# New transfer and GpSimd prices in a one-core decoder trunk's scheduler, with edits to a layer norm and a block-diagonal store

## The chip, the cores and the metric

One core of a Trainium2 chip runs the whole program. The time is the device time of one launch in microseconds (us). The kernel before was run three times.

## The reference, cut to what matters

Two post-norm layers over 1024 positions of width 1024, all in float32. Layer 0 mixes with a gated DeltaNet (8 heads of 128, chunks of 64), layer 1 with an S5 state-space scan; beside each runs a 4-head attention into 256 memory tokens. Each layer ends in a squared-ReLU MLP of 4096. The layer norms are the part that the change touches most plainly:

```python
def layer_norm(x, g, b):
    mu = jnp.mean(x, axis=-1, keepdims=True)
    var = jnp.mean(jnp.square(x - mu), axis=-1, keepdims=True)
    return (x - mu) * lax.rsqrt(var + 1e-5) * g + b
...
for i in range(2):
    mix, xq = gdn_mixer(x, ...) if i == 0 else s5_mixer(x, ...)
    cross = memory_attention(xq, mem, w_kv[i])
    h = jnp.concatenate([mix, cross], -1) @ w_o[i]
    x = layer_norm(ALPHA * x + h, ln1_g[i], ln1_b[i])
    f = jnp.square(jax.nn.relu(x @ mlp_w1[i])) @ mlp_w2[i]
    x = layer_norm(ALPHA * x + f, ln2_g[i], ln2_b[i])
```

Inside the DeltaNet a unit lower triangular system of 64 x 64 is solved per chunk and head. The kernel inverts the 32 x 32 diagonal blocks of it first.

## The kernel before, in words

**Matmuls.** A float32 product is three matmuls on rounded parts: every operand x is split into xh (ScalarE casts it to fp32r) and xl = x - xh (VectorE), and `mm3` (L397, L398, L399) adds xh*yh, xl*yh, xh*yl into one PSUM bank. The large products also use a seven-product scheme, whose sums and differences of blocks are formed on VectorE (`s`, `a1`, `u`, `p`, `hid`, L599, L690, L696, L768) and go through DRAM scratch (`hd`, `wsd`, `wod`, `osd`). A block is 128 x 512 float32, 256 KB.

**Stages by time in the profile.** Projections and memory keys (to 200 us), the DeltaNet's heads in recurrence with the next head's projections woven in (to 700), output projection with layer norm 1 and the first MLP blocks (700 to 810), the first MLP with the S5 tables and coefficients beside it (to 1380), layer norm 2 (to 1450), the S5 scan, attention and gate (to 1700), and the same output projection, layer norm and MLP for layer 1. The last 8 row tiles of 128 x 1024 (`mlp_last`) each get two half accumulations `tm`, which VectorE adds into `y` (L931), then `layer_norm`, then a store of the tile to the output.

**What sets the order.** The code only records instructions. `settle` (L62, called once at the end of `run`, L2277) then simulates the five queues with prices from `price` (L293) and writes out one order per engine, which is fixed by dependencies without semaphores. It takes, at each step, the instruction that can start soonest, and among those the one that is due first; TensorE's own recorded order is kept within `reach=40` us, others may start up to `ahead=70` us before they are due. A transfer's price is a length of 1.6 us plus its size over 300 GB/s (2 us more from GpSimd, 0.7 more for short runs), and `late` is added to when its data are there: a 256 KB load from SyncE is counted as 1.6 + 0.85 + `late`. `late` isn't part of when something is due. An engine executes its queue strictly in order, so an instruction whose operand isn't there holds up all that stand behind it.

**Layer norm (L493).** Two forms. The one of layer norm 1, with `junk`, sums on ScalarE (L502 for the mean, L505 for the squares, each over two halves), finishes the statistics on VectorE (L503, L506), and uses a gain that was multiplied by 32 beforehand (L2302), as it works with the sum over 1024 in place of the mean. The one of layer norm 2, without `junk`, takes VectorE's statistics (L509 twice, L510), adds 1e-5 on GpSimd (L511) and raises to -1/2 on GpSimd (L512). Then VectorE applies (y - mean) * gain (L515) and y * rstd + bias (L516).

**The diagonal blocks.** `gdn_keys_out` runs 16 times (8 heads, 2 halves). It leaves NT, the strict lower part, 4 tiles of 128 x 128. ScalarE copies the four 32 x 32 diagonal blocks into `pkd` (L1157, four copies of 32 x 128), and GpSimd issues one store of `pkd` to `ntd` (L1158) and one of the whole NT to `ntf` (L1159). `gdn_inverse` reads `ntd` for two heads at a time. On the same GpSimd queue stand the powers for the keys' and outputs' norms (L1140, L1452).

Of the kernel before, what the change touches and what calls it, by code (L numbers as in the profile page):

```python
# [20 lines left out]
HALF = 512  # L21
# [12 lines left out]
class Trunk:  # L34
# [258 lines left out]
    def price(self, i, big):  # L293

        E = mybir.EngineType
        if i.opcode == "DMACopy":
            def run(ap):
                k = 1
                for s, c in reversed(ap):
                    if s != k:  # L300
                        break
                    k *= c
                return 4 * k

# [12 lines left out]
        slow = 1.65 if any(s > 1 and c > 1 for s, c in q) else 1.0  # L317
        scalars = any(math.prod(c for s, c in x.bass_ap.ap[1:]) == 1 for x in i.ins if getattr(x, "bass_ap", None) is not None) and big > 1
        if i.engine == E.Activation:
            bank = self.home.get(i.ins[0].bass_ap.tensor.name, "s")[0] == "ps"  # L320
            if i.opcode == "TensorCopy":
                t = (0.05 if bank else 0.096) + 0.84e-3 * big * slow
            else:
                t = (0.08 if bank else 0.125) + 0.8e-3 * big + (0.08 if len(i.outs) > 1 else 0.0) + (0.07 if scalars else 0.0)
            return t, t + 0.1, 0
        if i.engine == E.Pool:
            t = 0.02 + 0.87e-3 * big if i.opcode == "Memset" else 0.5 if big < 2 else 1.0 if big < 8 else 0.17 + 2.1e-3 * big
            return t, t + 0.05, 0
        wide = sum(c > 1 for x in i.ins if getattr(x, "bass_ap", None) is not None for c in [math.prod(c for s, c in x.bass_ap.ap[1:])])
        if getattr(i, "is_tensor_tensor_scan", False):  # L330
            return 2.46e-3 * big, 2.46e-3 * big + 0.08, 0
        t = 0.07 + (0.53e-3 if i.opcode == "TensorScalarPtr" and wide < 2 else 1.04e-3) * big * slow + (0.06 if scalars and i.opcode == "TensorScalarPtr" else 0.0)
        return t, t + 0.08, 0
# [156 lines left out]
            out.append(t)  # L490
        return out

    def layer_norm(self, y, gb, junk=None):  # L493

        nc = self.nc
        st = self.tile("st", [P, 2, 6], F32, "bn")
        halves = y if isinstance(y, list) else [y[:, c * HALF:(c + 1) * HALF] for c in range(2)]
        mv = self.tile("st", [P, 4], F32, "mv")
        if junk is not None:
            s = st.rearrange("p a b -> p (a b)")  # L500
            for c in range(2):
                nc.scalar.activation(junk, halves[c], AF.Copy, accum_out=s[:, c:c + 1])  # L502
            nc.vector.tensor_scalar(mv[:, 0:1], s[:, 0:1], s[:, 1:2], -1.0 / 1024, op0=ALU.add, op1=ALU.mult)  # L503
            for c in range(2):
                nc.scalar.activation(junk, halves[c], AF.Square, bias=mv[:, 0:1], accum_out=s[:, 4 + c:5 + c])  # L505
            nc.vector.scalar_tensor_tensor(mv[:, 2:3], s[:, 4:5], s[:, 5:6], self.eps_ln, op0=ALU.add, op1=ALU.add)  # L506
        else:
            for c in range(2):
                nc.vector.bn_stats(st[:, c, :], halves[c])  # L509
            nc.vector.bn_aggr(mv[:, 0:2], st)  # L510
            nc.gpsimd.tensor_scalar(mv[:, 2:3], mv[:, 1:2], 1e-5, None, op0=ALU.add)  # L511
        nc.gpsimd.tensor_tensor(mv[:, 3:4], mv[:, 2:3], self.mhalf[:, 0:1], op=ALU.pow)  # L512
        parts = [(y, slice(0, 1024))] if not isinstance(y, list) else [(y[c], slice(c * HALF, (c + 1) * HALF)) for c in range(2)]
        for o, c in parts:
            nc.vector.scalar_tensor_tensor(o, o, mv[:, 0:1], gb[0][:, c], op0=ALU.subtract if junk is None else ALU.add, op1=ALU.mult)  # L515
            nc.vector.scalar_tensor_tensor(o, o, mv[:, 3:4], gb[1][:, c], op0=ALU.mult, op1=ALU.add)  # L516
# [603 lines left out]
    def gdn_keys_out(self, h, hf):  # L1120


        nc = self.nc
        V = nc.vector
        kT = self.kTs[h % 4]
        t4 = slice(4 * hf, 4 * hf + 4)
# [21 lines left out]
        n = self.tile("h1", [P, 4, P], F32, "NT")  # L1148
        for t in range(4):
            tt = 4 * hf + t  # L1150
            c = slice(tt * P, (tt + 1) * P)
            nc.tensor.matmul(pq[:, t, :], kT[:, c], kT[:, c], start=True, stop=True)
        V.scalar_tensor_tensor(n, pq, -1.0, d, op0=ALU.mult, op1=ALU.mult)
        pkd = self.tile("S", [P, 4, 32], F32, "pkd")
        for b in range(4):
            q = slice(32 * b, 32 * b + 32)
            nc.scalar.copy(pkd[q], n[q, :, q])  # L1157
        nc.gpsimd.dma_start(self.ntd[h, t4].rearrange("t b j i -> (b j) t i"), pkd)  # L1158
        nc.gpsimd.dma_start(self.ntf[h, hf], n)  # L1159

    def gdn_inverse(self, h0):
# [1041 lines left out]
    def run(self):  # L2203
        nc = self.nc
# [69 lines left out]
        for _ in steps:  # L2274
            pass
        self.mlp_block(1, B, ahead, self.x3, None, a["out"].rearrange("(n s) d -> s n d", s=8), None)
        self.settle(self.begin, self.nc.cur_bb.bb.instructions[-1], reach=40.0, ahead=70.0, margin=0.2, late=0.7)  # L2277

    def rows(self, src):

# [54 lines left out]
    def mlp_block(self, i, B, ahead, xd, side, out, more):  # L2335
        new = []

        def done(y, tau):
            if tau == 0:
                self.gb2 = self.load_gb(self.a["ln2_g"][i:i + 1], self.a["ln2_b"][i:i + 1])  # L2340
                if more:
                    new.extend(self.new_xT())
            self.layer_norm(y[tau], self.gb2)
            self.nc.sync.dma_start(out[tau], y[tau])
            if more and tau == 7:
                self.last_x(y, new, more(new))
            elif more and tau < 6:
                self.transpose_x(y[tau], tau, new)

        self.mlp_first(i, B, ahead, side)  # L2350
        self.mlp_second(i, xd, done, side)
        return new
# [87 lines left out]
```

## Time and profile before

| | |
|---|---|
| median of 3 runs | 2513.91 us (2511.46 to 2515.65) |
| the profiled execution, its time | 2513.31 us |
| its span | 2511.6 us (1.7 us lie around it) |
| TensorE busy | 2472.5 us, 98% of the span |
| VectorE busy | 1973.9 us, 79% |
| ScalarE busy | 1294.0 us, 52% |
| GpSimd busy | 420.7 us, 17% |
| moved by DMA | 481.18 MB |
| granted TensorE clock, mean | 0.999 |

How to read it: TensorE is busy nearly all the time, so what can be lost or won is the time in which it waits, 39 us of 2512, and what it takes from its last matmul to the end. The view of waits lists, for each engine, whom an instruction waited for with its sum, count and longest; a timeline row has its start and length, engine, line, operation, output<-inputs, and in brackets the idle time of the engine just before it with what ended it.

### The profile page before, as it was taken

Reading aid. Unit: us, or ns where it says so; the run is one execution under the profiler, and the core shown is the slowest. Engines: PE = TensorE matmul, PEld = TensorE weight load, DVE = VectorE, ACT = ScalarE, POOL = GpSimd, SP = SyncE. Lnnn points to the kernel's source line nnn. Section 1 sums busy time; section 2 is a strip of 40 time slices with the busy share of each in tenths; the row PEclk is TensorE's granted clock in tenths of the full one; section 3 lists DMA queues with packets and bytes.
Section 4 is the critical chain, followed back from the end, with each engine's and each line's share of the span. In section 5 each row is a group of like instructions: output and inputs, shape, how many; then the busy total and the mean of one; then the engine's idle time right before and its main releaser. Section 6 shows DMA issues by size and latency. Waiting matters only on the chain.

```text
span 2511.6 us, 36963 instructions
## 1 busy us (share of the span) xinstructions
PE 2472.5 (98%) x12181; PEld 2060.4 (82%) x12181; DVE 1973.9 (79%) x3663; ACT 1294.0 (52%) x2776; POOL 420.7 (17%) x641
## 2 busy tenths in 40 slices
PE   8999999999999999999999999999999999999998
PEld 6888888888887887888888888888887888888886
DVE  7786878888779798879988957776687666578788
ACT  6665565554456566554444244564365555544441
POOL 0132232314002023312210223112011000000001
PEclk9999999999999999999999999999999999999999
DMA  6453575767754567477454479669736444574532
GB/s 215 119 166 119 141 238 152 234 199 238 262 163 151 198 206 242 166 283 242 141 161 143 156 242 305 200 220 330 258 130 202 159 143 164 213 261 130 168 105 97
DMA packets 319089, 481.18 MB, mean 192 GB/s; under 512 B 109440, under 2 KB 139344, under 8 KB 318896
## 3 DMA queue, kind: packets, MB, share of 16 engines
q1 hardware_dynamic: 292912, 423.76, 51.5%
q0 software_dynamic: 23680, 50.85, 7.0%
q10 hardware_dynamic: 2304, 4.20, 0.5%
q8 instruction: 96, 1.57, 0.3%
q14 instruction: 97, 0.79, 0.1%
HBM read 321.91 MB, written 156.73 MB: 191 GB/s over the span
## 4 chain that ended last, share of the span: by engine, by line
PE 87%; DVE 5%; ACT 3%; DMA 2%; issue 2%; POOL 1%; SPq 0%; POOLq 0%; DVEq 0%; ACTq 0%
PE q L398 7%; PE q L399 7%; PE q L397 7%; PE pA L399 4%; PE pA L397 4%; PE pA L398 4%; PE tm L397 4%; PE tm L398 4%; PE tm L399 4%; PE wi L397 3%; PE wi L399 3%; PE wi L398 3%; PE pC L399 2%; PE pC L397 2%; PE pC L398 2%
## 5 line engine op out<-in xcount | busy, mean ns | idle before, releaser
L397 PE MATMUL q<-wkh,hkh 128*128 128x512 f32 x784 | 306.2, 391 | 0.8 <-ACT G L1881 0.8
L398 PE MATMUL q<-wkl,hkh 128*128 128x512 f32 x784 | 306.0, 390 | 0.5 <-DVE wkl L894 0.5
L399 PE MATMUL q<-wkh,hkl 128*128 128x512 f32 x784 | 305.3, 390 | 0.0
L893 ACT CAST wkh<-wr 128x512 fp32r<-128x512 f32 x168 | 104.8, 624 | 238.0 <-PE q L398 185.8
L397 PEld LDWEIGHTS q<-wkh,hkh 128*128 128x128 f32 x784 | 147.2, 188 | 32.5 <-ACT G L1881 1.7
L398 PEld LDWEIGHTS q<-wkl,hkh 128*128 128x128 f32 x784 | 147.2, 188 | 31.1 <-DVE wkl L894 1.1
L399 PEld LDWEIGHTS q<-wkh,hkl 128*128 128x128 f32 x784 | 147.2, 188 | 30.2
L894 DVE TENSOR_TENSOR wkl<-wr,wkh 128x512 fp32r<-128x512 f32 x168 | 115.4, 687 | 65.6 <-issue 56.5
L397 PE MATMUL wi<-xTh,wih 128*128 128x512 f32 x384 | 158.0, 411 | 1.6 <-ACT qT L1091 1.6
L398 PE MATMUL wi<-xTl,wih 128*128 128x512 f32 x384 | 153.1, 399 | 0.0
L399 PE MATMUL wi<-xTh,wil 128*128 128x512 f32 x384 | 152.9, 398 | 0.0
L894 DVE TENSOR_TENSOR hkl<-hr,hkh 128x512 fp32r<-128x512 f32 x196 | 133.8, 683 | 0.1
L893 ACT CAST hkh<-hr 128x512 fp32r<-128x512 f32 x196 | 120.8, 616 | 2.6 <-DMA hr<-hd 2.6
L511 POOL TENSOR_SCALAR mv<-mv 128x1 f32<-128x1 f32 x16 | 9.0, 565 | 631.6 <-DVE mv L510 631.6
L397 PE MATMUL tm<-so 128*128 128x512 f32 x280 | 110.3, 398 | 0.4 <-ACT so L1616 0.4
L1616 ACT CAST so<-or 128x1024 fp32r<-128x1024 f32 x70 | 71.9, 1051 | 61.4 <-DMA or<-wod 40.0
L1617 DVE TENSOR_TENSOR so<-or,so 128x1024 fp32r<-128x1024 f32 x70 | 84.3, 1220 | 19.4 <-ACT so L1616 17.4
L399 PE MATMUL tm<-so 128*128 128x512 f32 x224 | 87.8, 393 | 0.0
L398 PE MATMUL tm<-so 128*128 128x512 f32 x224 | 87.7, 392 | 0.0
L397 PEld LDWEIGHTS wi<-xTh,wih 128*128 128x128 f32 x384 | 72.9, 190 | 14.4 <-ACT qT L1091 2.0
L399 PEld LDWEIGHTS wi<-xTh,wil 128*128 128x128 f32 x384 | 72.6, 189 | 14.0
L398 PEld LDWEIGHTS wi<-xTl,wih 128*128 128x128 f32 x384 | 72.8, 190 | 11.8 <-issue 0.2
(582 smaller groups left out, 7389.8 us busy)
## 6 DMA issues: line engine op xcount, KB each, us to landing
hr<-hd SPq DMA_DIRECT2D x212, 256.0 KB, 2.8
wr<-in_w_dram SPq DMA_DIRECT2D x56, 512.0 KB, 4.8
hd<-u SPq DMA_DIRECT2D x92, 256.0 KB, 2.0
w1r<-in_w_dram SPq DMA_DIRECT2D x32, 512.0 KB, 3.6
hd<-hid SPq DMA_DIRECT2D x60, 256.0 KB, 2.4
hd<-p SPq DMA_DIRECT2D x60, 256.0 KB, 2.1
w1r<-in_w_dram SPq DMA_DIRECT2D x56, 256.0 KB, 3.6
wir<-in_w_in_dram SPq DMA_DIRECT2D x24, 512.0 KB, 4.0
```

The lines of the kernel that those rows point to most:

```text
L397: mm(ps, a[0], b[0], start=start, stop=False, skip_group_check=onto)
L398: mm(ps, a[0], b[1], start=False, stop=False, skip_group_check=onto)
L399: mm(ps, a[1], b[0], start=False, stop=stop, skip_group_check=onto)
L511: nc.gpsimd.tensor_scalar(mv[:, 2:3], mv[:, 1:2], 1e-5, None, op0=ALU.add)
L893: nc.scalar.copy(hi, s)
L894: nc.vector.tensor_tensor(lo, s, f32(hi), op=ALU.subtract)
L1616: nc.scalar.copy(hi, r)
L1617: V.tensor_tensor(lo, r, f32(hi), op=ALU.subtract)
```

## The change

Three kinds of edits are made at once.

1. Prices. `late` goes from 0.7 to 1.5 us, so each transfer is taken to land 0.8 us later. A GpSimd tensor-tensor operation on one column is priced 0.9 us in place of 0.5.
2. Layer norm 2. The `1e-5` step moves from GpSimd to VectorE and works on 1024 times the variance (the gain is multiplied by 32 on ScalarE, once per layer). In layer 1, tiles 5 and 6 use the form with ScalarE's sums, with a free PSUM bank as scratch. The very last tile applies the bias in two halves, each with a store of its own.
3. Diagonal blocks. The copies into `pkd` are gone; four stores per call take the blocks out of NT directly.

```diff
         if i.engine == E.Pool:
-            t = ... else 0.5 if big < 2 else 1.0 if big < 8 else 0.17 + 2.1e-3 * big
+            t = ... else (0.9 if i.opcode == "TensorTensor" else 0.5) if big < 2 else 1.0 if big < 8 else 0.17 + 2.1e-3 * big
...
-    def layer_norm(self, y, gb, junk=None):
+    def layer_norm(self, y, gb, junk=None, last=None):
...
             nc.vector.bn_aggr(mv[:, 0:2], st)
-            nc.gpsimd.tensor_scalar(mv[:, 2:3], mv[:, 1:2], 1e-5, None, op0=ALU.add)
+            nc.vector.tensor_scalar(mv[:, 2:3], mv[:, 1:2], 1024.0, 1024 * 1e-5, op0=ALU.mult, op1=ALU.add)
         nc.gpsimd.tensor_tensor(mv[:, 3:4], mv[:, 2:3], self.mhalf[:, 0:1], op=ALU.pow)
+        if last is not None:
+            nc.vector.scalar_tensor_tensor(y, y, mv[:, 0:1], gb[0], op0=ALU.subtract, op1=ALU.mult)
+            for c in range(2):
+                c = slice(c * HALF, (c + 1) * HALF)
+                nc.vector.scalar_tensor_tensor(y[:, c], y[:, c], mv[:, 3:4], gb[1][:, c], op0=ALU.mult, op1=ALU.add)
+                nc.sync.dma_start(last[:, c], y[:, c])
+            return
...
-        pkd = self.tile("S", [P, 4, 32], F32, "pkd")
         for b in range(4):
             q = slice(32 * b, 32 * b + 32)
-            nc.scalar.copy(pkd[q], n[q, :, q])
-        nc.gpsimd.dma_start(self.ntd[h, t4].rearrange("t b j i -> (b j) t i"), pkd)
+            nc.gpsimd.dma_start(self.ntd[h, t4, b].rearrange("t j i -> j t i"), n[q, :, q])
...
-        self.settle(..., reach=40.0, ahead=70.0, margin=0.2, late=0.7)
+        self.settle(..., reach=40.0, ahead=70.0, margin=0.2, late=1.5)
...
                 self.gb2 = self.load_gb(self.a["ln2_g"][i:i + 1], self.a["ln2_b"][i:i + 1])
+                self.nc.scalar.activation(self.gb2[0], self.gb2[0], AF.Copy, scale=32.0)
...
-            self.layer_norm(y[tau], self.gb2)
-            self.nc.sync.dma_start(out[tau], y[tau])
+            self.layer_norm(y[tau], self.gb2, self.psum("mm", "jk") if tau in ((), (5, 6))[i] else None, last=out[tau] if tau == 7 and not more else None)
+            if tau < 7 or more:
+                self.nc.sync.dma_start(out[tau], y[tau])
```

The count of TensorE's instructions stays the same. Its order is the same for most of the program: of every hundred matmuls, ten stand more than seven places from where they stood, mostly in the DeltaNet's recurrence and around the two layer norms 1. The other engines' orders are reshuffled locally. Line numbers after the edits are 5 to 7 higher (L599 becomes L606, L573 L580, L931 L938, L516 L523, L1140 L1147, L1159 L1164).

**VectorE in the first MLP, near 932 us.** Before, `hid` is added to `p` between the two sums `s` of one coefficient, and the low part `a1l` comes behind:

```order
L765 TENSOR_TENSOR p_1829_10445<-pB_10556,p_1829_10445 128x512
L696 TENSOR_TENSOR s_1837_10521<-w1r_10517,w1r_10518 128x512
L599 TENSOR_TENSOR hid_10489<-hid_10489,p_1794_10224 128x512
L690 TENSOR_TENSOR s_1838_10523<-s_1837_10521,w1r_10515 128x512
L573 TENSOR_TENSOR a1l_10526<-w1r_10515,a1h_10525 128x512
L573 TENSOR_TENSOR s1l_10530<-s_1837_10521,s1h_10529 128x512
L768 TENSOR_TENSOR u_1831_10475<-pA_10432,u_1831_10475 128x512
```

The same block of the first MLP (same tiles under new numbers) in the changed kernel's VectorE queue:

```order
L703 TENSOR_TENSOR s_1821_10489<-w1r_10485,w1r_10486 128x512
L772 TENSOR_TENSOR p_1813_10413<-pB_10524,p_1813_10413 128x512
L697 TENSOR_TENSOR s_1822_10491<-s_1821_10489,w1r_10483 128x512
L580 TENSOR_TENSOR a1l_10494<-w1r_10483,a1h_10493 128x512
L580 TENSOR_TENSOR s1l_10498<-s_1821_10489,s1h_10497 128x512
L775 TENSOR_TENSOR u_1815_10443<-pA_10400,u_1815_10443 128x512
L606 TENSOR_TENSOR hid_10457<-hid_10457,p_1778_10192 128x512
```

The step on `hid` moved from ahead of `a1l` to behind it. This holds in some blocks and is reversed in others.

**VectorE at the end of the program.** `tm` is a half accumulation from TensorE, `mv_24311` belongs to tile 6 and `mv_24349` to tile 7, the last. Before:

```order
L515 SCALAR_TENSOR_TENSOR y_21743<-y_21743,mv_24311,gb_24078 128x1024
L931 TENSOR_TENSOR y_21743<-tm_24320,y_21743 128x512
L516 SCALAR_TENSOR_TENSOR y_21743<-y_21743,mv_24311,gb_24080 128x1024
L509 BN_STATS bn_24348<-y_21743 128x6
L931 TENSOR_TENSOR y_21743<-tm_24334,y_21743 128x512
L509 BN_STATS bn_24348<-y_21743 128x6
L510 BN_AGGR mv_24349<-bn_24348 128x2
L515 SCALAR_TENSOR_TENSOR y_21743<-y_21743,mv_24349,gb_24078 128x1024
L516 SCALAR_TENSOR_TENSOR y_21743<-y_21743,mv_24349,gb_24080 128x1024
```

In the changed kernel the same queue ends like this (`mv_24285` is tile 6's, `mv_24325` tile 7's):

```order
L503 TENSOR_SCALAR mv_24285<-bn_24284 128x1
L938 TENSOR_TENSOR y_21712<-tm_24296,y_21712 128x512
L509 BN_STATS bn_24324<-y_21712 128x6
L506 SCALAR_TENSOR_TENSOR mv_24285<-bn_24284,eps_ln 128x1
L522 SCALAR_TENSOR_TENSOR y_21712<-y_21712,mv_24285,gb_24047 128x1024
L938 TENSOR_TENSOR y_21712<-tm_24310,y_21712 128x512
L523 SCALAR_TENSOR_TENSOR y_21712<-y_21712,mv_24285,gb_24049 128x1024
L509 BN_STATS bn_24324<-y_21712 128x6
L510 BN_AGGR mv_24325<-bn_24324 128x2
L514 SCALAR_TENSOR_TENSOR y_21712<-y_21712,mv_24325,gb_24047 128x1024
L511 TENSOR_SCALAR mv_24325<-mv_24325 128x1
L517 SCALAR_TENSOR_TENSOR y_21712<-y_21712,mv_24325,gb_24049 128x512 x2
```

Tile 6's bias step (L523) now stands behind the last addition of `tm` and still ahead of the last tile's statistics; the variance step L511 stands behind the 1024-wide L514.

**GpSimd in the DeltaNet's recurrence, fourth head.** Before:

```order
L1159 DMA ntf<-NT_2451 128x512
L1158 DMA ntd<-pkd_2457 128x4x32
L1140 TENSOR_TENSOR scr_79<-scr_79,half 128x4
L1452 TENSOR_TENSOR scr_79<-scr_79,mhalf 128x4
L1159 DMA ntf<-NT_2553 128x512
L1158 DMA ntd<-pkd_2559 128x4x32
```

After:

```order
L1163 DMA ntd<-NT_2439 32x4x32 x4
L1164 DMA ntf<-NT_2439 128x512
L1147 TENSOR_TENSOR scr_79<-scr_79,half 128x4
L1457 TENSOR_TENSOR scr_79<-scr_79,mhalf 128x4
L1163 DMA ntd<-NT_2539 32x4x32 x4
L1164 DMA ntf<-NT_2539 128x512
```

Four issues stand where one stood, ahead of the store of NT instead of behind it, and the powers follow them.

More of the change, by code (lines that the diff above doesn't have):

```diff
@@ L326, in price @@
         if i.engine == E.Pool:
-            t = 0.02 + 0.87e-3 * big if i.opcode == "Memset" else 0.5 if big < 2 else 1.0 if big < 8 else 0.17 + 2.1e-3 * big
+            t = 0.02 + 0.87e-3 * big if i.opcode == "Memset" else (0.9 if i.opcode == "TensorTensor" else 0.5) if big < 2 else 1.0 if big < 8 else 0.17 + 2.1e-3 * big
             return t, t + 0.05, 0
@@ L2276, in run @@
         self.mlp_block(1, B, ahead, self.x3, None, a["out"].rearrange("(n s) d -> s n d", s=8), None)
-        self.settle(self.begin, self.nc.cur_bb.bb.instructions[-1], reach=40.0, ahead=70.0, margin=0.2, late=0.7)
+        self.settle(self.begin, self.nc.cur_bb.bb.instructions[-1], reach=40.0, ahead=70.0, margin=0.2, late=1.5)
     def rows(self, src):
```

## The prediction

> **What bounds the kernel now.** I read the page first, then the busy time by stage, then TensorE's waits, then the timeline at the longest waits and at the end. The page says who is full:
>
> ```profile
> span 2511.6 us, 36963 instructions
> PE 2472.5 (98%) x12181; PEld 2060.4 (82%) x12181; DVE 1973.9 (79%) x3663; ACT 1294.0 (52%) x2776; POOL 420.7 (17%) x641
> ```
>
> TensorE is idle for 2511.6 - 2472.5 = 39.1 us. The change leaves its 12181 matmuls as they are, so their 2472.5 us stay, and only the 39 us can move much. Where they lie, from the view by stretches (start:end, length, then busy time of PE, PEld, DVE, ACT, POOL):
>
> ```profile
> 0.00:10.00 10.00, 2.47 (x6) 1.23 (x7) 3.33 (x8) 4.38 (x6) 1.76 (x14) 1.00 0.74 261
> ...
> 200.00:600.00 400.00, 391.69 (x2208) 330.81 (x2207) 324.66 (x668) 223.80 (x713) 121.00 (x186) 1.00 0.63 183
> ...
> 700.00:810.00 110.00, 107.09 (x517) 86.13 (x517) 91.83 (x144) 66.96 (x139) 20.90 (x18) 1.00 0.48 158
> ...
> 900.00:1000.00 100.00, 96.85 (x425) 79.16 (x424) 90.38 (x243) 66.53 (x118) 37.84 (x68) 1.00 0.71 228
> ...
> 2460.00:2512.00 52.00, 41.91 (x185) 34.36 (x184) 46.07 (x65) 0.00 (x0) 10.69 (x16) 0.93 0.20 81
> ```
>
> 7.5 us are the start (the change doesn't reach it), 10.1 us the end. The middle holds 39.1 - 7.5 - 10.1 = 21.5 us: 8.3 in the DeltaNet's recurrence, 2.9 at layer norm 1, 3.2 in the first MLP's tables, some 7 spread over the rest. The granted clock is full in all of them. TensorE's waits, the longest in total (sum, times, longest):
>
> ```profile
> PE pA L399 <- DVE a1l L573: 3.1, 2, 1.7
> PE wi L397 <- ACT qT L1091: 1.6, 1, 1.6
> PE pA L399 <- DVE w1l L364: 1.5, 2, 1.0
> ...
> PE wz L397 <- ACT vT L1091: 1.3, 2, 0.8
> ...
> PE pS L1436 <- ACT e L1432: 1.1, 3, 0.7
> ```
>
> No single wait exceeds 1.7 us, and each ends with VectorE or ScalarE coming late to an operand. These two are busy for 79% and 52%, so this is lateness in an in-order queue and no lack of engine. That is what another order can mend, or make.
>
> **The change part by part.**
>
> *Transfers counted as landing later.* The scheduler counts 1.6 + 0.85 + 0.7 = 3.15 us for a 256 KB load from SyncE before, 3.95 after; for 512 KB 4.0 and 4.8. What they took (size, median us from issue to landing):
>
> ```profile
> hr<-hd SPq DMA_DIRECT2D x212, 256.0 KB, 2.8
> wr<-in_w_dram SPq DMA_DIRECT2D x56, 512.0 KB, 4.8
> or<-wod SPq DMA_DIRECT2D x40, 256.0 KB, 3.7
> x<-y SPq DMA_DIRECT2D x32, 256.0 KB, 2.1
> ```
>
> The old price fits the quick ones, the new price the slow ones. The longest wait of the profile, at 932 us, shows what a slow one does:
>
> ```profile
> 932.17 0.69 DVE L599 TENSOR_TENSOR hid<-hid,p 128x512 f32<-128x512 f32 x1 [1.59 <-DMA hd<-hid]
> 932.78 0.68 DVE L690 TENSOR_TENSOR s<-s,w1r 128x512 f32<-128x512 f32 x1
> 933.38 0.68 DVE L573 TENSOR_TENSOR a1l<-w1r,a1h 128x512 fp32r<-128x512 f32 x1
> ...
> 934.12 0.50 PE L399 MATMUL pA<-xB,a1l 128*128 128x512 f32 x1 [1.68 <-DVE a1l L573]
> ```
>
> VectorE stands 1.59 us before `hid`, because an earlier store of that buffer hasn't been read out; behind it stand the second `s` and `a1l`, and TensorE waits 1.68 us for `a1l`. In the new order `hid` stands behind `a1l`: 1.59 us of the 1.68 go. What is late next there is `hid` itself, which only stores a sum, so nothing near it waits. Term: -1.6 us. Against it stands that in other blocks, three in this MLP and four in the second at most, `hid` now stands two to four places ahead of `a1l` where it was behind. A store that is late there would cost the same 1.6 us; before, three blocks stood so and one waited. For the rest of the middle I take a smaller value: the waits on `w1l` (1.5) and the second one on `a1l` (1.4) lie behind loads or tables and gain at most the 0.8 us by which their estimates grow, so from -1.6 to 0 for the two, and +1.6 if the order swaps them for others. I take -0.8.
>
> *The diagonal blocks.* Rows of the tiles `pkd` and `ntd`, and of 32-partition loads on GpSimd's queue (duration in ns: least, median, most):
>
> ```profile
> L1157 ACT COPY pkd<-NT x64: 280/295/300, 53.6 to 507.5; 32x128 f32<-32x128 f32 x64
> L1158 POOL DMA_DIRECT2D ntd<-pkd x16: 750/762/824, 60.4 to 508.1; - x16
> ...
> L1274 POOL DMA_DIRECT2D iv<-t x64: 548/549/615, 156.4 to 591.7; - x64
> ```
>
> ScalarE loses 64 x 0.295 = 18.9 us of work, all between 54 and 508 us. Each group of four held its queue for 1.18 us just after NT, ahead of evacuations like `qT`, `vT` and `e`, for which TensorE waits 1.6 + 1.3 + 1.1 = 4.0 us in this stage. GpSimd gains: four issues at 0.549 are 2.20 in place of 0.762, +1.43 us, 16 times, +22.9 us in a stage where it is busy for 121 of 400 us. Along the path from NT to `ntd` the two cancel (1.18 + 0.76 before, 2.20 after). Four ScalarE copies less ahead of the evacuations is worth between 0 and the 4.0 us; an evacuation is behind such a group only some of the time, and the reshuffle of this stage (where TensorE's own order moves most) can also cost. I take -2.5. Cover for GpSimd's longer issues is its idle 70%; where the powers L1140 and L1452 stand right behind them, that cover is gone and each costs up to 1.43 us (a rival, below).
>
> The Trainium skill's page "SBUF — State Buffer", section "SBUF: two separate sides", speaks against putting more issues on GpSimd: while VectorE runs an operation that takes both ports, GpSimd cannot write its descriptors, and the transfer starves. The rows of L1274 don't show that: with VectorE busy for 325 of 400 us, the longest of 64 issues took 0.615 against a median of 0.549, so by the trace the sum stays as it is.
>
> *Layer norm 2 and the end.* The last tile before, and TensorE's last matmul of the last two halves:
>
> ```profile
> 2498.80 0.39 PE L399 MATMUL tm<-w2h,hk 128*128 128x512 f32 x1
> ...
> 2501.52 0.39 PE L399 MATMUL tm<-w2h,hk 128*128 128x512 f32 x1
> ```
>
> ```profile
> 2502.99 0.68 DVE L931 TENSOR_TENSOR y<-tm,y 128x512 f32<-128x512 f32 x1
> ...
> 2504.43 0.21 DVE L510 BATCH_NORM_AGGREGATE mv<-bn 128x2 f32<-128x12 f32 x1
> 2504.67 1.28 DVE L515 SCALAR_TENSOR_TENSOR y<-y,mv,gb 128x1024 f32<-128x1024 f32 x1
> 2504.73 1.31 POOL L511 TENSOR_SCALAR mv<-mv 128x1 f32<-128x1 f32 x1 [3.58 <-DVE mv L510]
> 2506.12 0.57 POOL L512 TENSOR_TENSOR mv<-mv,mhalf 128x1 f32<-128x1 f32 x1
> 2506.72 1.28 DVE L516 SCALAR_TENSOR_TENSOR y<-y,mv,gb 128x1024 f32<-128x1024 f32 x1 [0.77 <-POOL mv L512]
> 2508.03 0.33 SPq L2344 DMA_DIRECT2D out_dram<-y  x1
> ```
>
> The last addition starts 1.1 us after TensorE ends (2501.9), since VectorE is still at tile 6. From L510 to L516 it takes 2.29 us. In the new order L511 stands on VectorE behind the 1024-wide L514: 0.24 to L514, 1.2 for it, 0.2 for L511, about 0.3 to GpSimd, 0.57 for the power: 2.5 us, so moving L511 gains nothing here, because it was put behind the operation that blocked it before. Tiles 5 and 6 now go through ScalarE, whose steps have these lengths (layer norm 1's rows; squares of two halves, then VectorE):
>
> ```profile
> 779.58 0.72 ACT L505 ACTIVATE tw<-y,mv 128x512 bf16<-128x512 f32 x1
> ...
> 781.05 0.19 ACT L505 ACTIVATION_READ_ACCUMULATOR tw<-y,mv 128x1 f32 x1
> ...
> 781.27 0.22 DVE L506 SCALAR_TENSOR_TENSOR mv<-bn,eps_ln 128x1 f32<-128x1 f32 x1 [0.77 <-ACT tw L505]
> ```
>
> 1.7 us for the squares, by the same kind of pass some 0.8 for the sum of the half that came last, and 0.3 at each handover. TensorE makes a half in 2501.52 - 2498.80 = 2.72 us, so tile 6's second half is there at 2496.5. VectorE reaches its addition behind tile 5's two 1.2 us steps, about 2498.0 by these lengths; the sum is ready at 2499.5, the squares at 2501.5, L522 ends at 2502.8. Then in order the last addition (0.6), tile 6's L523 (1.2), half the statistics (0.6), L510 at 2505.3 instead of 2504.4, and with 2.5 us the first L517 at 2507.8. Its second half ends at 2509.0 (2508.0 before), but its store has 256 KB, 2.1 us against 2.7 for 512 KB by the kinds of rows above (the second, by its group):
>
> ```profile
> x<-y SPq DMA_DIRECT2D x8, 512.0 KB, 2.7
> ```
>
> Term: +1.0 - 0.6 = +0.4 us. Bounds: -0.8 if VectorE is at tile 6 as soon as TensorE, +1.5 if each ScalarE handover costs 0.3 more. In layer 0 the same step moves and the extra gain scaling is one 128 x 1024 pass per layer, asked for tens of us after its load: nothing, with 0.5 us either way.
>
> *Sum.* -1.6 - 0.8 - 2.5 + 0.4 = -4.5 us by the parts that I can name. To this I add -1.2 for the other 7 us of scattered waits, a sixth of them, on the ground that a later landing only ever moves a consumer back behind work that is ready; between -4 and +4, since an order can also put two late things in a row. That is -5.7. The profiled execution took 2513.31, 0.6 us below the median: 2513.31 - 5.7 = 2507.6, and 2508.2 against the median. I say 2508.0. About 0.2% (5.0 us: 2508.9 to 2518.9 is no change) is what a measurement of this kernel can tell from nothing.
>
> **The rivals.**
>
> *The waits only change places* (2513 us, 2509 to 2519). For it: TensorE's order is nearly the old one, all gains are of 1 or 2 us, the end gives a little back, and half of the 21.5 us (layer norms' serial chains, the recurrence) isn't about transfers. Against it: the one wait whose rows I could follow in the new order goes.
>
> *GpSimd's queue becomes the wait* (slower). Place: 200 to 600 us, the powers behind the four issues. Price 1.43 us each, up to 22.9 us for 16. It decides by the number of calls in which a power is asked for within 1.43 us behind the issues: four such calls (4 x 1.43 = 5.7) eat the whole gain, eight (11.4 against 5.7 + 5.0 = 10.7) make it slower than can be mistaken. If ScalarE's 2.5 us don't come either, nine give 12.9 - 5.7 + 2.5 = +9.7, 2523 us, and twelve 2527. For it: both powers follow directly in the new order. Against it: GpSimd is 70% idle there, and the scheduler prices these issues at 0.6 us, above the rows' 0.549, so it has planned for them.
>
> *`hid` ahead of `a1l`* (slower). Seven blocks times 1.6 us is 11.2, less the 1.6 won: 2523 us, with half of them 2518. Against it: one of three waited before, and only where the tables' transfers were thick.
>
> **How the numbers follow.** Waits shrink as summed, by 5 us or more: 0.40, with a range of its own of 2499 to 2508.9. Places change: 0.33. GpSimd's queue: 0.15. `hid` and like collisions: 0.12. So faster 0.40, the same 0.33, slower 0.27. The low end of the range is the sum with the best value of each part: -1.6 - 1.6 - 4.0 - 0.8 - 4 = -12, 2501.5, which I round to 2501; the upper end is 2523, where both slower cases have their middle. About 1 in 10 is left out on each side.
>
> **What would show it.** Right: no wait of over 1 us for `a1l` in the first MLP; less than 6 us idle between 200 and 600; L511 on VectorE behind L514 and the last store 2.1 us long; the end between 9 and 11 us after TensorE's last matmul. Wrong: TensorE idle for 10 us or more between 200 and 600, with the powers' starts on GpSimd pushed behind the stores of the blocks; new waits for `a1l` behind `hid`; or more idle time at the layer norms 1 than the 2.9 us.

## The result: 13 us slower

| | before | after |
|---|---|---|
| median | 2514.36 us (6 runs, 2511.46 to 2515.65) | 2527.49 us (6 runs, 2524.97 to 2528.06) |
| profiled execution, its span | 2513.31, 2511.6 us | 2527.54, 2525.8 us |
| TensorE's last matmul ends at | 2501.9 us | 2515.9 us |
| granted TensorE clock, mean | 0.999 | 0.994 |

The ratio is 1.0053, 95% interval 1.0042 to 1.0064: slower by 10.6 to 16.1 us. Forecast were 2508.0 us and, at most, 2523.

The page of the changed kernel, its first lines:

```profile
span 2525.8 us, 36952 instructions
PE 2479.4 (98%) x12181; PEld 2069.0 (82%) x12181; DVE 1975.3 (78%) x3676; ACT 1289.0 (51%) x2732; POOL 435.8 (17%) x673
```

The same 12181 matmuls are busy for 6.9 us more (2479.4 against 2472.5), and TensorE is idle for 46.4 us where it was idle for 39.1. A busy time that grows without more work is the first thing to see: some of the matmuls ran slower. The stretches, as in the prediction:

```profile
200.00:600.00 400.00, 390.23 (x2181) 332.18 (x2179) 320.71 (x666) 211.04 (x668) 129.01 (x208) 0.99 0.64 186
700.00:810.00 110.00, 106.56 (x507) 87.16 (x506) 90.10 (x139) 66.03 (x141) 21.75 (x19) 0.97 0.47 158
900.00:1000.00 100.00, 100.00 (x443) 82.81 (x442) 94.08 (x249) 69.97 (x124) 38.07 (x71) 1.00 0.74 237
2460.00:2526.00 66.00, 55.24 (x243) 45.10 (x241) 57.59 (x91) 14.57 (x31) 7.26 (x8) 0.96 0.24 93
```

The first MLP's tables (900 to 1000) are now full, as forecast; the granted clock (third number from the end) is below 1.00 in two stages where it was full, and layer norm 1 (700 to 810) is idle for 3.4 us instead of 2.9. TensorE's waits, from the same view as before:

```profile
PE ba L1011 <- ACT xTh L993: 7.6, 2, 7.3
PE ks L1429 <- DVE S L1446: 4.4, 2, 3.6
PE tm L397 <- ACT so L1621: 3.7, 1, 3.7
PE xt L530 <- DVE xB L535: 3.0, 3, 1.5
PE tm L397 <- DVE y L894: 1.9, 2, 1.2
PE tm L399 <- DVE ow L1654: 1.7, 1, 1.7
```

The waits for `a1l` and `w1l`, together 4.6 us before, are gone from the head of the list. In their place stand two of 3.6 and 3.7 us, where nothing in the middle of the program had waited longer than 1.7.

**Where the 14 us arise.** The starts of the same matmul in both traces, subtracted (us; the first column is its time before; the next is how much later it starts in the changed kernel):

| matmul | before | after | e1 edits only | e2 late back | e4 prices only | e9 chain early |
|---|---|---|---|---|---|---|
| last `ks` of the recurrence | 691.7 | +4.8 | +1.3 | +2.9 | +6.0 | +3.7 |
| last `xt` of layer 0 (norm 1 done) | 804.3 | +7.3 | +1.0 | +3.1 | +8.4 | +6.0 |
| first `wu` (layer 1 begins) | 1431.7 | +2.6 | -1.0 | -0.3 | +5.4 | +0.9 |
| first `so` product of layer 1 | 1750.2 | +3.7 | -1.9 | -0.7 | +6.5 | +1.3 |
| last `xt` of layer 1 | 1909.0 | +13.4 | -2.3 | +1.2 | +16.5 | +1.3 |
| end of the last matmul | 2501.9 | +14.0 | -2.5 | +1.1 | +17.1 | +2.2 |

So the changed kernel loses 4.8 us in the recurrence and 2.5 in the first output projection with layer norm 1, wins 4.7 back in the first MLP, loses 1.1 in the S5 part, and then loses 9.7 us in the second output projection alone. (e1 to e9 are experiments, below. Executions differ by up to 2.4 us in such a row even with the same work in the same order: +4.8, +7.2 and +6.1 at the last `ks` for the changed kernel, e5 and e11, whose TensorE runs the same list up to there. One difference shows: a power on GpSimd near 441 us took 1.1 us in the changed kernel's profile and 3.2 us in the other two.)

**The wait near 1795 us.** The timeline of the changed kernel, rows of SyncE's queue, VectorE, ScalarE and TensorE in order of time:

```profile
1777.86 0.43 SPq L623 DMA_DIRECT2D ws<-cat  x1
...
1784.17 0.68 DVE L630 TENSOR_TENSOR ws<-ws,ws 128x512 f32<-128x512 f32 x1
...
1784.88 0.32 SPq L635 DMA_DIRECT2D osd<-ws  x1
...
1789.65 0.32 SPq L1615 DMA_DIRECT2D or<-osd  x1
1790.01 0.43 SPq L1616 DMA_DIRECT2D or<-wod  x1
...
1794.76 1.04 ACT L1621 CAST so<-or 128x1024 fp32r<-128x1024 f32 x1 [12.02 <-DMA or<-wod]
...
1795.86 0.51 PE L397 MATMUL tm<-so 128*128 128x512 f32 x1 [3.70 <-ACT so L1621]
```

It is a chain: four blocks are loaded into `ws`, VectorE forms the seven-product scheme's sums in place (L630 to L633), SyncE stores them to the scratch `osd`, and half of the product's operand `or` is loaded back from there (the other half comes from `wod`, one issue behind). The product that waits reads the first of this last group's four sums. Before, the same chain (other line numbers) had this time:

```profile
1764.58 0.43 SPq L616 DMA_DIRECT2D ws<-cat  x1
...
1771.40 0.68 DVE L623 TENSOR_TENSOR ws<-ws,ws 128x512 f32<-128x512 f32 x1
...
1772.12 2.06 SPq L628 DMA_DIRECT2D osd<-ws  x2
...
1776.21 0.47 SPq L1611 DMA_DIRECT2D or<-wod  x1
...
1782.90 0.50 PE L397 MATMUL tm<-so 128*128 128x512 f32 x1 [0.35 <-ACT so L1616]
```

The last load into `ws` is issued 13.3 us later than before, the first sum and its store come 12.8 us later, the load of `or` 13.8 us, and TensorE starts the product 13.0 us later; only 3.7 of these were there when the stage began. From the first sum to the product it takes 11.7 us, 11.5 before: inside this group next to nothing is lost. The delay had grown over the groups ahead, which go through the same few `ws` buffers: the first sums of the five groups stand at 1711.5, 1725.3, 1738.9, 1756.0 and 1771.4 before, and 6.9, 11.8, 17.2, 13.4 and 12.8 us later in the changed kernel. The chain was just hidden before, with nothing to spare: TensorE already waited 0.35 us for it.

Of the 9.7 us, 6.2 are waits (TensorE is idle for 8.6 us in this stretch, 2.4 before; 3.7 and 0.8 of them for `so`, 1.7 for `ow`). The other 3.4 are the clock, half of the 6.8 us that it stood at half (shown below).

**Half the clock behind the waits.** The view by stretches of 4 us, around both long waits (columns as in the prediction: the clock is the third number from the end):

```profile
434.00:438.00 4.00, 0.58 (x3) 0.16 (x1) 4.00 (x12) 1.94 (x3) 0.49 (x1) 1.00 0.22 63
438.00:442.00 4.00, 3.36 (x14) 3.10 (x14) 3.85 (x10) 2.74 (x9) 3.98 (x6) 0.50 0.87 229
442.00:446.00 4.00, 3.43 (x13) 2.80 (x13) 3.96 (x8) 2.75 (x14) 3.71 (x7) 0.50 0.75 233
446.00:450.00 4.00, 4.00 (x22) 3.61 (x20) 1.28 (x5) 1.93 (x9) 4.00 (x8) 0.72 0.61 161
450.00:454.00 4.00, 4.00 (x23) 3.32 (x22) 1.40 (x3) 0.86 (x2) 4.00 (x9) 1.00 0.74 195
...
1798.00:1802.00 4.00, 4.00 (x11) 3.03 (x11) 3.62 (x5) 2.77 (x4) 0.00 (x0) 0.50 0.51 184
1802.00:1806.00 4.00, 4.00 (x16) 3.23 (x15) 4.00 (x5) 1.69 (x2) 0.00 (x0) 0.83 0.84 248
1806.00:1810.00 4.00, 4.00 (x20) 3.30 (x19) 0.53 (x1) 1.12 (x2) 0.00 (x0) 1.00 0.82 282
```

TensorE is "busy" for 4.00 of 4.00 us from 1798 on and yet starts 11 matmuls where it starts 20 at full clock. That is the busy time which grew. By the trace's record the clock was at half from 438.0 to 448.2, from 803.2 to 810.1 (at two waits of 1.5 and 1.0 us for `xB` at layer norm 1) and from 1796.5 to 1803.3 us. In the kernel before it was full from 12.6 us to the end of its last matmul.

**The wait at 434 us.** VectorE in the changed kernel:

```profile
434.75 1.28 DVE L1233 TENSOR_TENSOR pr<-X,st 128x512 f32<-128x512 f32 x2
435.95 1.27 DVE L1235 TENSOR_REDUCE X<-pr 128x32 f32<-128x512 f32 x2
...
437.75 0.34 DVE L1446 SCALAR_TENSOR_TENSOR S<-S,scr,pS 128x128 f32<-128x128 f32 x1
...
438.15 0.80 PE L1429 MATMUL ks<-S,kT 128*128 128x128 f32 x2 [3.56 <-DVE S L1446]
```

The last rounds of the inverse's products (L1233, L1235) fill VectorE without a gap from 426.1 to 437.2, and the recurrence's update S stands behind them. Before, they ended at 432.4, while TensorE still had other products to do.

### The profile page after: what moved, and what is told of

Read it like the earlier page. It is cut to its first block, busy times and chain, and to the rows that moved or that the text cites. A ratio compares the mean times of both kernels' runs of the same rounds, so it can differ in the third digit from the quotient of the medians.

```text
span 2525.8 us, 36952 instructions
## 1 busy us (share of the span) xinstructions
PE 2479.4 (98%) x12181; PEld 2069.0 (82%) x12181; DVE 1975.3 (78%) x3676; ACT 1289.0 (51%) x2732; POOL 435.8 (17%) x673
## 4 chain that ended last, share of the span: by engine, by line
PE 88%; DVE 4%; ACT 2%; DMA 2%; issue 2%; POOL 1%; SPq 0%; DVEq 0%; POOLq 0%; ACTq 0%
PE q L398 7%; PE q L399 7%; PE q L397 7%; PE pA L397 4%; PE pA L399 4%; PE pA L398 4%; PE tm L398 4%; PE tm L397 4%; PE tm L399 4%; PE wi L397 3%; PE wi L398 3%; PE wi L399 3%; PE pC L397 2%; PE pC L399 2%; PE pC L398 2%; PE pB L397 2%
## 5 line engine op out<-in xcount | busy, mean ns | idle before, releaser
L397 PE MATMUL q<-wkh,hkh 128*128 128x512 f32 x784 | 306.7, 392 | 0.2
L399 PE MATMUL q<-wkh,hkl 128*128 128x512 f32 x784 | 305.4, 390 | 0.0
L512 POOL TENSOR_TENSOR mv<-mv,mhalf 128x1 f32<-128x1 f32 x32 | 27.8, 867 | 871.2 <-DVE mv L511 631.4
L397 PEld LDWEIGHTS q<-wkh,hkh 128*128 128x128 f32 x784 | 147.2, 188 | 32.3 <-ACT G L1886 1.0
L399 PEld LDWEIGHTS q<-wkh,hkl 128*128 128x128 f32 x784 | 147.2, 188 | 30.3
L397 PE MATMUL wi<-xTh,wih 128*128 128x512 f32 x384 | 159.0, 414 | 0.6 <-ACT qT L1098 0.6
L399 PE MATMUL wi<-xTh,wil 128*128 128x512 f32 x384 | 153.3, 399 | 0.0
L397 PE MATMUL tm<-so 128*128 128x512 f32 x280 | 110.2, 401 | 3.7 <-ACT so L1621 3.7
L399 PE MATMUL tm<-so 128*128 128x512 f32 x224 | 87.9, 394 | 0.0
L399 PEld LDWEIGHTS wi<-xTh,wil 128*128 128x128 f32 x384 | 72.5, 189 | 14.3
L397 PEld LDWEIGHTS wi<-xTh,wih 128*128 128x128 f32 x384 | 72.8, 190 | 12.4 <-ACT qT L1098 0.8
```

What stands on the lines that cost most here:

```text
L397: mm(ps, a[0], b[0], start=start, stop=False, skip_group_check=onto)
L399: mm(ps, a[1], b[0], start=False, stop=stop, skip_group_check=onto)
```

## Experiments

Two theories stood first: the landing price `late` makes the loss (L), or the edits do (E). A third was kept beside them: that any new order is another draw (D). All ratios are to the kernel before, run on the same chip in the same session.

| run | what it is | median us | ratio (95%) |
|---|---|---|---|
| e1 | edits, prices of before | 2512.81 | 0.9993 (0.9984 to 1.0002) |
| e2 | changed kernel, `late` 0.7 | 2514.70 | 1.0000 (0.9991 to 1.0009) |
| e3 | changed kernel, GpSimd price 0.5 | 2528.07 | 1.0055 (1.0042 to 1.0067) |
| e4 | before, both new prices | 2528.73 | 1.0054 (1.0040 to 1.0068) |
| e5 | `late` 1.5 in the first 700 us only | 2517.90 | 1.0015 (1.0006 to 1.0024) |
| e6 | `late` 1.5 behind 700 us only | 2523.87 | 1.0042 (1.0028 to 1.0055) |
| e7 | 1.5 for the data only | 2525.34 | 1.0047 (1.0034 to 1.0059) |
| e8 | 1.5 for freeing buffers only | 2514.64 | 1.0008 (0.9999 to 1.0016) |
| e9 | transfers of `osd` and `ws` at 0.7, rest 1.5 | 2516.67 | 1.0010 (1.0002 to 1.0019) |
| e10 | transfers of `osd` and `ws` at 1.5, rest 0.7 | 2520.76 | 1.0029 (1.0019 to 1.0038) |
| e11 | zero matmuls in the wait | 2526.82 | 1.0053 (1.0039 to 1.0066) |
| e12 | changed kernel, 1.5 in the first MLP only, rest 0.7 | 2511.89 | 0.9991 (0.9982 to 1.0000) |
| e13 | GpSimd's transfers at 0.7, rest 1.5 | 2527.87 | 1.0052 (1.0040 to 1.0064) |
| e14 | changed kernel, `late` 1.1 | 2518.26 | 1.0011 (1.0002 to 1.0020) |
| e15 | changed kernel, `late` 0.3 | 2519.49 | 1.0015 (1.0006 to 1.0025) |
| e16 | e12 with the GpSimd price 0.5 | 2512.64 | 0.9989 (0.9980 to 0.9997) |

**Which part of the change (e1 to e4).**

```diff
-        self.settle(..., margin=0.2, late=1.5)     # e1, e2: after
+        self.settle(..., margin=0.2, late=0.7)
-            ... (0.9 if i.opcode == "TensorTensor" else 0.5) if big < 2     # e1, e3: after
+            ... 0.5 if big < 2
```

e4 makes the reverse edits in the kernel before.

> The edits to layer norm 2 and to the diagonal blocks, with the prices of before (late 0.7, one-column GpSimd operations 0.5). If the late landing price makes the loss (theory L): about before minus the small terms of the prediction, 2509 to 2514 us, and neither of the two long waits of the changed kernel (3.6 us for ks at 434 us, 3.7 us for tm at 1796 us). If the edits make it (theory E, four GpSimd issues and the norm's new steps): 2525 to 2529 us with the 434 us wait there. If any new order is simply another draw (theory D): anything between 2508 and 2528, with long waits at other places.

> The changed kernel with late back at 0.7, all else as changed. Theory L: 2509 to 2515 us, both long waits gone. Theory E: 2525 to 2529 us. Theory D: not tied to either; it need not agree with the run of the edits alone, though only the price of GpSimd's one-column operations differs.

> The changed kernel with the one-column GpSimd price back at 0.5, late at 1.5. Theory L: 2525 to 2529 us, both long waits stay. If the GpSimd price pushes the recurrence's update S back behind the inverse's products (theory P): the wait at 434 us goes and the time falls by about 7 us, to 2520 us. Theory D: a few us either way with waits elsewhere.

> The kernel before with both new prices and none of the edits. Theory L: 2521 to 2529 us, with the wait for tm near 1790 us there. Theory E: 2511 to 2516 us. Theory D: anything between 2508 and 2528; the changes of the edits alone and of the prices alone would not add up to 13 us.

The kernels with `late` at 1.5 are 13 to 15 us slower, with the edits or without; both with 0.7 are where the kernel before is. Theory E falls. The GpSimd price alone accounts for nothing that can be measured (e3 against the changed kernel). The wait near 1795 us comes with the price alone (from the waits of e4):

```profile
PE tm L397 <- ACT so L1616: 4.4, 1, 4.4
```

The wait for `ks` doesn't: e4 has none longer than 0.2 us, but one of 4.6 us for `vT` at 444 us in its place.

The edits do have a cost of their own in the recurrence, by the mechanism of a rival in the prediction. e1, e2, e6, e12 and e16, whose TensorE and VectorE run the same lists up to 700 us, end it 1.3, 2.9, 3.3, 2.2 and 4.2 us later than the one profile of before. e1 on GpSimd and ScalarE:

```profile
433.37 2.23 POOL L1163 DMA_DIRECT2D ntd<-NT  x4
435.62 1.29 POOL L1457 TENSOR_TENSOR scr<-scr,mhalf 128x4 f32<-128x4 f32 x1
...
436.94 1.14 ACT L1460 ACTIVATE on<-po,scr 128x128 f32<-128x128 f32 x4 [2.66 <-POOL scr L1457]
```

Four issues stand ahead of the power, ScalarE waits 2.66 us for it, and TensorE then 2.4 us for `on`. It happens in full at this one place, not at nine: the five waits for `on` of e1 sum to 4.1 us.

**Where (e5, e6).** The planned start r of a transfer chooses its price:

```diff
-                    length = served - r + late
+                    length = served - r + (1.5 if r < 700 else 0.7)     # e6: the other way round
```

> The changed kernel with the late landing of 1.5 us only for what the scheduler starts in its first 700 us (the DeltaNet's part), 0.7 behind that. Theory L1 (two separate places, each with its own wait): the wait for ks at 434 us stays, that for tm near 1790 us goes; about 7 us above the kernel with late back at 0.7, so 2519 to 2523 us. Theory D (each new order is another draw): not tied to the two waits; anything between 2508 and 2530.

> The changed kernel with late 0.7 in the scheduler's first 700 us and 1.5 behind. Theory L1: no wait for ks at 434 us, the wait of 3.7 us for tm near 1790 us and the one of 1.7 us for ow near 1830 us stay; about 10 us above the kernel with late back, 2522 to 2527 us. Together with the run of the first part the two losses should add up to 12 to 16 us. Theory D: no such sum.

The losses are 5.2 and 11.1 us (2517.90 and 2523.87 against 2512.75), together 16.3 where the whole change loses 13.1: two places, adding up within the intervals. e5 has the wait for `ks` of 3.6 us and none for `so`; e6 has the wait for `so` of 4.0 us and none for `ks`. e5 came out a little lower than expected. The second part holds a smaller place too: at layer norm 1 TensorE waits 2.5 us for `xB` in the changed kernel and 2.7 in e6, but 0.9 us in e5.

**Data or buffers (e7, e8).** The scheduler uses `late` for when data can be read and for when a buffer comes free:

```diff
-     over[nm] = max(over[nm], r + length + ...)
+     over[nm] = max(over[nm], r + length - (0.8 if moves else 0.0) + ...)     # e7; e8: late=0.7 and + 0.8
```

> The changed kernel with late 1.5 for when a transfer's data can be used, but 0.7 for when a buffer that a transfer reads or writes comes free. If the loss comes from consumers being put back behind other work (theory C): 2523 to 2529 us, both long waits stay. If it comes from buffers taken to be free later, so that loads are issued later (theory R): 2512 to 2517 us, the wait near 1790 us goes, since the loads of ws come back to where they stood.

> The other half: late 0.7 for the data and 1.5 for when buffers come free. Theory C: 2512 to 2517 us. Theory R: 2523 to 2529 us with the wait for tm near 1790 us.

The time follows the data (theory C). But the wait for `so` in e7 is 1.1 us, as theory R had it: the long wait needs both. e7 loses its 6.0 us of the second projection in waits of at most 1.3 us (5.4 us, 2.4 before) and in two stretches of 3.4 us at half the clock behind them, another 3.4. A theory that names one wait for the whole loss would be wrong.

**The chain (e9, e10).**

```diff
-                    length = served - r + late
+                    length = served - r + (0.7 if any(nm.startswith(('osd', 'ws_')) for nm in uses(ins[x])) else 1.5)
```

e10 swaps the two numbers. The rule reaches further than the chain: `ws` is also the name of the buffers in which the weights' sums for `wsd` and `wod` are made, and 144 of its 244 transfers lie in the first 700 us.

> The changed kernel with late 0.7 for the transfers that touch the scratch osd or its buffers ws (load of four blocks, store of their sums, load back as or), and 1.5 for all others. Theory K (the second projection loses through this chain, in which one transfer waits for the other, so that 0.8 us count three times over): the wait of 3.7 us for tm near 1790 us goes, and with it most of the 10 us of that stage; 2515 to 2520 us. Theory G (the loss is general, from all consumers put back): 2524 to 2529 us.

> The converse: 1.5 for the transfers that touch osd or ws, 0.7 for all others. Theory K: about 10 us above the kernel with late back, 2521 to 2526 us, lost between the first so of layer 1 and its last transposes. Theory G: 2513 to 2517 us.

With these transfers priced as before, the second projection loses nothing (+1.3 at its start and at its end, in the table above; 9.7 in the changed kernel), the first sums of its five groups come only 1.5 to 3.5 us late, the longest wait for `so` is 0.9 us, and the whole is 3 us above before instead of 13: theory K, though for all sums that go through `ws` together; the chain through `osd` wasn't priced by itself. The converse run is less clean. With only these late, the five sums come 6.3 to 13.1 us late, nearly as in the changed kernel, but the longest wait for `so` is 1.1 us and the second projection loses 4.2 us (from +3.1 to +7.3), not 10. The recurrence ends at +7.8, where `ws` is late too. So this price is what moves the chain and is needed for the large loss, but is not enough alone: which of the other transfers turn the late chain into the waits of 3.7 us for `so` and 1.7 for `ow`, and so into the half clock, isn't settled.

**The clock (e11).** Fourteen matmuls with zero weights stand in the wait, everything else in the same order:

```diff
+     for _ in range(14):
+         nc.tensor.matmul(ps, self.zz, X[0][0][:, R], start=False, stop=False)
...
```

> The changed kernel with 14 more matmuls (128x512, weights all zero, so they add nothing to the bank) right ahead of the tm matmul that waits 3.7 us near 1790 us; everything else in the same order. They take 14 x 0.227 = 3.2 us of the wait. Theory H (behind a wait of this length TensorE runs at half the clock for some 7 us, and that is lost on top): the granted clock stays at 1.00 behind the wait and 3 to 4 us are saved, 2523 to 2525 us. Theory N (what follows is paced by the loads of or, so that the clock there costs nothing): 2526 to 2529 us with clock 1.00 and more waits for so.

The rows of e11 (L1642 are the added matmuls; L404 to L406 are the former L397 to L399) and the clock there:

```profile
1793.41 3.41 PE L1642 MATMUL tm<-so,zz 128*128 128x512 f32 x14
1796.66 0.40 PE L404 MATMUL tm<-so 128*128 128x512 f32 x1
1797.82 0.50 PE L405 MATMUL tm<-so,so 128*128 128x512 f32 x1 [0.76 <-DVE so L1629]
...
1800.00:1804.00 4.00, 3.94 (x17) 2.71 (x16) 4.00 (x6) 2.13 (x3) 0.00 (x0) 1.00 0.76 226
```

The clock stays full. From the matmul that waits 0.76 us to the projection's last `so` product it is 77.6 us here (1797.82 to 1875.44) and 80.1 in the changed kernel (1797.12 to 1877.17), with the same waits in both: 2.4 us were lost to the clock there, in these two executions, less than theory H's 3 to 4. In the whole time, 2526.82 against 2527.49, that can't be told from nothing.

**Is a higher price good anywhere, and is 1.5 just bad luck (e12 to e16).** The line of e5 again, and `late` for e14 and e15:

```diff
-                    length = served - r + late
+                    length = served - r + (1.5 if 760 < r < 1410 else 0.7)     # e12, e16
+                    length = served - r + (0.7 if e == E.Pool else 1.5)        # e13
...
+        self.settle(..., margin=0.2, late=1.1)     # e14; e15: late=0.3
```

> The edits with late 1.5 only for what the scheduler starts between its 760 and 1410 us (first MLP and the S5 tables), 0.7 elsewhere. If the later landing is a gain there, as forecast (no waits for a1l): the stretch from the last transposes of layer 0 to the first q matmul takes 2 to 4 us less than before, and the whole 2509 to 2513 us, faster than both kernels. If the gain there only made up for time lost ahead of it (theory M): 2513 to 2516 us, as with late back.

> The changed kernel with late 0.7 for GpSimd's own transfers and 1.5 for SyncE's and ScalarE's. If the recurrence loses through the inverse's transfers on GpSimd's queue (theory Q): the wait for ks at 434 us shrinks by 2 us or more, the recurrence ends 3 us earlier than in the changed kernel, 2523 to 2525 us. If through SyncE's (theory S): 2526 to 2529 us. The wait near 1790 us stays in both.

> The changed kernel with late 1.1, half way. If the loss grows with the price (theory L): 2518 to 2523 us, with the wait near 1790 us there but shorter than 3.7 us. Theory D: anything between 2508 and 2528, not between the two neighbours.

> The changed kernel with late 0.3. Theory L carried on downwards: 2509 to 2514 us, no long wait in the second projection, waits on loads elsewhere that come later than priced. If a price below what transfers take costs as much as one above (theory V, a best value in between): 2516 to 2522 us. Theory D: anything.

> The edits, late 1.5 for what the scheduler starts between its 760 and 1410 us and 0.7 elsewhere, and the one-column GpSimd price back at 0.5. If the parts add up: 1 to 2 us below the same kernel with the price of 0.9, 2509 to 2512 us. If the GpSimd price has no part in the time: 2511 to 2513 us.

Over 0.3, 0.7, 1.1 and 1.5 the ratio is 1.0015, 1.0000, 1.0011 and 1.0053, with waits for `so` of 0.9, 0.8, 1.6 and 3.7 us. Only 1.5 stands clear: the other three lie within the 0.2% that counted as no change. Their order fits theory L above 0.7 and theory V below, but shows neither. What may cost at 0.3 isn't shown by one place: TensorE waits 2.6 us in four waits for `a1l`, but e14 has 2.8 of these too. Theory D would have allowed such a row of four values, but doesn't explain why the losses of e5 and e6 add up, nor why e3, e4 and e13 agree with the changed kernel.

e13 shrinks the wait for `ks` to 2.0 us, but its recurrence ends about as late as the changed kernel's (+5.9 at the last `ks`) and the time stays: theory S by the total, with other waits taking over. The higher price costs the recurrence about 3 us (the mean of the three values with 1.5 is +6.0; the three kernels with 0.7 there and the same GpSimd price, e2, e6 and e12, have +2.9, +3.3 and +2.2). Through which of SyncE's transfers stays open; e8 and e10 have a wait of 2.7 us for `ks` too.

In e12 the first MLP has almost no wait for `a1l` left (0.2 us; 3.1 before). From the last `xt` of layer 0 to the first `wu` it gains 3.9 us, but with 0.7 there e2 gains 3.4, e1 2.0 and e5 1.3: against e2 the higher price is worth half a microsecond, and the spread leaves its size open. e12 and e16 have the lowest ratios, 0.1% below the kernel before, e16 with an interval that just excludes 1; both are within the 0.2% that counted as no change and can't be told from e1.

## Why the prediction was wrong

- **The term for scattered waits is the step that failed.** It was "-1.2 for the other 7 us of scattered waits ... on the ground that a later landing only ever moves a consumer back behind work that is ready; between -4 and +4". The ground was false. Where transfers follow each other (load, sums, store, load, and the next group through the same buffers), the price counts again at each, and what moves back is not a consumer but the *issue* of the next transfer. The second projection, with one wait of 0.35 us for `so` before, got +9.7 us; it had no term of its own. By e9 the price on the sums' transfers is needed for that; that it counts once per transfer fits the delay's growth over the groups, but wasn't measured transfer by transfer. The rows that could have warned were the chain's: the load of `or` at 1776.21, the wait of 0.35 us at 1782.90.
- **A wait was priced too low.** New waits were taken at up to 1.6 us, the size of those seen. The new ones were 3.6 and 3.7 us, and behind each the clock halved, a loss that the sum had no term for: the busy time of the 12181 matmuls, which the prediction held fixed, grew by 6.9 us. The stretch rows of before show the middle at 1.00 throughout.
- **The first MLP, -2.4: right in kind.** `a1l` and `w1l` no longer hold TensorE there and the stage gains 4.7 us. The argument on `hid` put this down to the higher price; by e2 and e12 that price is worth half a microsecond of it, by e1 and e5 more; it isn't settled.
- **The diagonal blocks, -2.5: wrong in sign, as far as one profile of before can tell.** With the prices of before the recurrence ends 1.3 us later (e1), not earlier; over the five runs with its order it is 2.8 us in the mean. The waits for `qT`, `vT` and `e` shrink, but `on` waits behind GpSimd's issues. That was the second rival, at one place of 2.4 us instead of nine.
- **The price of the issues: right; the sign of the idle time: not.** The 64 issues take 0.551 us in the median (forecast 0.549). TensorE is idle for 9.8 us between 200 and 600, just below the 10 us set as a sign against, but far above the 6 set as a sign for, and busy time there includes a stretch at half clock. The sign against at layer norm 1 came too: 3.4 us idle instead of 2.9.
- **The end, +0.4: right in its steps.** From the end of the last matmul to the end of the span it is 9.9 us, 9.7 before: +0.2. L511 stands behind L514, L510 comes 0.8 us later after TensorE's end than before (0.9 forecast), L510 to L517 takes 2.32 us (2.5 forecast), and the last store lands 2.0 us after its issue (2.1 forecast):

```profile
2519.17 0.21 DVE L510 BATCH_NORM_AGGREGATE mv<-bn 128x2 f32<-128x12 f32 x1
2519.41 1.28 DVE L514 SCALAR_TENSOR_TENSOR y<-y,mv,gb 128x1024 f32<-128x1024 f32 x1
2520.62 0.14 DVE L511 TENSOR_SCALAR mv<-mv 128x1 f32<-128x1 f32 x1
2520.91 0.55 POOL L512 TENSOR_TENSOR mv<-mv,mhalf 128x1 f32<-128x1 f32 x1 [3.76 <-DVE mv L511]
2521.49 1.42 DVE L517 SCALAR_TENSOR_TENSOR y<-y,mv,gb 128x512 f32<-128x512 f32 x2 [0.73 <-POOL mv L512]
```

- **The rivals.** The likeliest slower case needed many small waits; what came were two large places, one of them a chain that no rival named. The first rival's remark, that half of the idle time isn't about transfers, was right for the kernel before and said nothing of the kernel after.

## What to carry to other kernels

In a kernel whose first engine is 98% full, a scheduler's price that is moved towards caution has little to win and can lose at the chains that have no slack left: before such a change, look for transfers that feed transfers, count the price for each of them and for each group that reuses their buffers, and compare the sum with the slack in the trace of before. A price should be changed where it is wrong, for the queue, chain or stage whose rows say so, and not for every transfer. And a wait of several microseconds on TensorE is to be charged with the slow stretch behind it, 2.4 us in e11's comparison.

## What the runs showed of the hardware

TensorE's waits and its clock go together, but the length of one wait doesn't decide. Behind 1.68 us (before, 934 us, and after, 1832 us) the clock stayed at 1.00. Behind 2.93 us (e1, 573 us) it fell to half for 3.4 us, and behind 3.70 us for 6.8, until 1803, 6 us after the matmuls had become dense again at 1797. Yet two waits of 1.08 and 0.76 us close together (e7, 1797 us) were followed by 3.4 us at half as well. e1 in stretches of 4 us:

```profile
571.00:575.00 4.00, 1.40 (x6) 0.92 (x6) 4.00 (x8) 1.01 (x4) 1.16 (x2) 0.93 0.62 187
575.00:579.00 4.00, 3.54 (x16) 3.29 (x17) 3.61 (x7) 2.15 (x5) 2.88 (x5) 0.64 0.91 243
579.00:583.00 4.00, 4.00 (x25) 3.49 (x24) 2.23 (x7) 0.43 (x3) 3.86 (x8) 1.00 0.52 112
```

The same waits can end either way. Near 803 us the changed kernel and e11 run the same lists and have the same two waits of 1.5 and 1.0 us; the changed kernel is at half from 803.2 us on for 6.8 us, e11 not at all. The changed kernel, then e11, in stretches of 3 us:

```profile
801.00:804.00 3.00, 0.66 (x4) 0.42 (x4) 3.00 (x6) 1.64 (x3) 2.10 (x2) 0.87 0.84 268
804.00:807.00 3.00, 2.97 (x14) 2.87 (x15) 2.21 (x4) 1.28 (x3) 2.42 (x3) 0.50 0.94 343
...
801.00:804.00 3.00, 1.48 (x9) 0.92 (x7) 3.00 (x5) 1.18 (x2) 1.56 (x1) 1.00 0.54 184
804.00:807.00 3.00, 1.95 (x14) 1.26 (x12) 2.83 (x5) 1.67 (x3) 2.08 (x4) 1.00 0.87 304
```

In all these traces the stretches at half inside the program last 3.4, 6.8 or 10.2 us.

The Trainium skill's page "TensorE: Matmul & The Clock Gate", Part 1, states that idling for a window of about 3.4 us takes the clock to half and that a busy window of the same length brings it back. The halving is what the rows show, though already behind 2.93 us, and in e7 behind 1.08 and 0.76; the way back took one, two or three times 3.4 us.

Matmuls whose weights are all zero kept the clock up in e11's wait: it stayed at 1.00.
